# Finer last groups and early modulation reads in stage one, a stepped gate chain, and unscaled down sums in a hybrid retention/mLSTM step on one core

## The chip, the cores and the metric

The kernel runs on one core of a Trainium2 chip. The metric is the device time of one launch in microseconds. A core has a matrix engine (PE), three engines for elementwise work (DVE, ACT, POOL), an engine whose queue issues most transfers (SP), and 16 DMA engines. Each engine takes its instructions in the order of the program and waits at the first one whose inputs or buffers are not ready. PSUM is the memory in which PE leaves its sums.

## The reference

One layer on 384 tokens of 2048 features: 128 context tokens (v = 0) and 256 latent tokens (v = 1). Two conditioning vectors give, through `w_mod`, six vectors for each of them, which shift, scale and gate the layer.

```
mod = silu(c) @ w_mod + b_mod                     # per v: sh1, sc1, g1, sh2, sc2, g2
h   = ln(x) * (1 + sc1) + sh1
proj = h @ w_in                                   # 2048 x 8208, the last 16 columns are gates
ret  = retention in both directions, 4 heads, rope on q and k of the latent tokens
mls  = mLSTM in both directions, 4 heads, with cumulative sums of log_sigmoid(gates)
mix  = concat(ln(ret)*gn*silu(rg), sigmoid(mo)*ln(mls)*gn) @ w_out
x1   = ln(ALPHA * x + g1 * mix) * ln1_g + ln1_b
h2   = ln(x1) * (1 + sc2) + sh2
u, g = split(h2 @ w_up)                           # 2048 x 11008
y    = ln(ALPHA * x1 + g2 * ((silu(conv3(u)) * g) @ w_down)) * ln2_g + ln2_b
```

The final retention and mLSTM states of the context tokens are outputs too. All data are float32. A product is made of three matmuls: each factor is split into a high part `hi` (a copy in the matmul's rounded format, on ACT, L117) and the rest `lo` (a subtraction, on DVE or POOL, L118), and hi*hi, hi*lo and lo*hi are summed in PSUM.

## The kernel before

**Names.** `raw` is a weight tile as it was read, `hi` and `lo` its halves, `ah`/`al` those of the activations, `fah`/`fal` those of the FFN's activations. `psa` are sums of q and k (128 x 384), `psb` sums of v and output gate (128 x 512), `psu` those of `w_up`, `psd` those of `w_down`. A row of features, 128 of 2048, is a "kt"; there are 16.

**Stage one** computes sh1 and sc1 and multiplies heads 0 and 1 while it does. Group (k0, n) covers kt k0 to k0+n-1. For a group, the generator `mods` reads 2 x 16 blocks of `w_mod` (tile `wm`), multiplies them with the conditioning vectors on PE (`modps`, L255), turns the result to columns (`mr`, `modf`, L264) and adds the bias on DVE (`sh`, `sc`, L267). `hs` then makes h (DVE, L337) and splits it (`ah`, `al`). `units` reads `w_in` for the two heads, multiplies the group's kt, and adds the sums to q, k, vx and og (`spill`, L397). In the loop over groups a Stepper advances `mods` of the next group between the units of this one, `finish` drains it, and `hs` of the next group follows after the group's units. Its reads run two tiles ahead (`lag` 2, four `wm` buffers).

**Behind it** come the tables (`cs`, `gnr`, on POOL's queue), rope on heads 0 and 1, the gates, and the other heads. For the gates the weights of the 16 gate columns are read (L552), multiplied with all 16 kt (`gps`, L559, 32 matmuls), summed (`gsum`, L564), passed through log_sigmoid, selected by rows (`gsel`, L575), scanned, and turned to columns (`gcp`). All of this is written in one piece ahead of head 2.

**Vectors by rows.** g1, sh2, sc2 and g2 are computed without PE. `mod_vector` reads 16 tiles `mraw` of `w_mod` for 1024 columns, and DVE multiplies each by the two conditioning values and adds it to `macc` (L283, L286: a pair of operations for each tile); PE sums over the partitions (`modr`). The result goes to DRAM (`modrow`) and is read back. `mods2` is the Stepper for parts 2 to 4, stepped in the projections of heads 2 to 7. `mods5` is that for g2, two blocks of 16 tiles, stepped in the first `ups`.

**Stage three** is the FFN. `ups` multiplies by `w_up`, convolves (L345, L349, L1095) and splits the result; `down` multiplies by `w_down` and `residual` adds g2 times the sum to the residual rows r (L885, L887, L890), with `g2b` as g2 spread over all partitions. The last part, `last_down`, has its own operations on r (L1174 to L1176), and then the final norm (L910 to L916) and the output.

**What sets the order.** The code is written as above, but a scheduler places each instruction on its engine by the readiness it works out, so reads and DVE's work of `mods2` and `mods5` can be placed ahead of the step that issues them in the code. `share_splits(n)` gives every n-th `lo` to POOL. SP's queue holds the reads of weights, of `wm` and of `mraw` in one line.

Of the kernel before, what the change touches and what calls it, by code (L numbers as in the profile page):

```python
# [9 lines left out]
F32 = mybir.dt.float32  # L10
# [72 lines left out]
def hybrid_step(ctx, tc, ca, cb, x_prompt, x_sample, state_ret, state_c, state_n, state_m, c, c_ctx,  # L83
# [294 lines left out]
    groups = [(0, 1), (1, 1), (2, 2), (4, 2), (6, 2), (8, 4), (12, 4)]  # L378
# [20 lines left out]
    def units(k0, n):  # L399
        for h in range(2):  # L400
# [17 lines left out]
    with ExitStack() as p0:  # L418
        xp = pool("xp", 3, p0)
# [10 lines left out]
        def group_raws(gs):  # L430
            return mod_loads(lambda: wmp.tile([P, 2048], F32, tag="wm", name="wm"),
                             [(q, KT // n, part * D + k0 * P, n * P) for k0, n in gs for part in range(2)
                              for q in range(0, KT, KT // n)], 2)

        first_raws, later_raws = group_raws(groups[:1]), group_raws(groups[1:])
# [25 lines left out]
        for kt in range(KT):  # L461
# [6 lines left out]
            if kt == 0:  # L468
                hs(0)
        for g in range(len(groups)):  # L470
            wide = g + 1 < len(groups) and groups[g + 1][1] == 4
            nxt = Stepper(mods(g + 1) if g + 1 < len(groups) else iter(()), 2.0 if wide else 1.2)
# [3 lines left out]
            if g + 1 < len(groups):  # L476
                hs(g + 1)


    with p1:  # L480
        tab = pool("tab", 1, p1, reuse_waits="tile")
        mp = pool("mp1", 3, p1, reuse_waits="tile")
        gx = ExitStack()
        gp = pool("gp", 1, gx, reuse_waits="tile")
        with tc.issue_after(on_pool[0]):
# [18 lines left out]
        pc = pat.tile([P, 64], F32, tag="ps", name="cps")  # L504
        for t in range(3):
            transpose(pc[:, t * 16:(t + 1) * 16], cqr[:, t, :], 16)
        transpose(pc[:, 48:64], n0r, 16)
        nc.vector.tensor_copy(cqw.rearrange("p t f -> p (t f)"), pc[:, 0:48])
        nc.vector.tensor_copy(n0c, pc[:, 48:64])
        ncol = tab.tile([P, 16], F32, name="ncol")  # L510

        def log_sigmoid(dst, x, shape, tg):
            def tmp(n):
                return gp.tile(shape, F32, tag=f"ls{tg}{n}", name=f"ls{tg}{n}")
            e, u, ln = tmp(0), tmp(1), dst
# [12 lines left out]
        log_sigmoid(lgb, lth, [P, 8], "t")  # L528
# [22 lines left out]
        raw = wraw.tile([P, 1024], F32, tag="raw", name="raw")
        nc.sync.dma_start(out=raw[:, :256].rearrange("p (k n) -> p k n", n=16),  # L552
                          in_=wi[:, 8192:8208].rearrange("(k p) n -> p k n", p=P))
        gw = whi.tile([P, 1024], F32R, tag="hi", name="gw")[:, :512].rearrange("p (k s n) -> p k s n", s=2, n=16)
        split(gw[:, :, 0], gw[:, :, 1], raw[:, :256].rearrange("p (k n) -> p k n", n=16), split_engine())
        gps = pmm.tile([32, T], F32, tag="ps", name="gps")
        for kt in range(KT):
            for h in (act_hi[kt], act_lo[kt]):
                nc.tensor.matmul(gps, lhsT=gw[:, kt].rearrange("p s n -> p (s n)"), rhs=h,  # L559
                                 start=kt == 0 and h is act_hi[0], stop=kt == KT - 1 and h is act_lo[kt])  # L560
        gpt = wraw.tile([P, 1024], F32, tag="raw", name="gpt")[:32, :T]
        nc.scalar.copy(gpt, gps)
        gps = pat.tile([16, T], F32, tag="ps", name="gsum")
        nc.tensor.matmul(gps, lhsT=cst[:32, C_SUM:C_SUM + 16], rhs=gpt, start=True, stop=True)  # L564
        gts = gp.tile([16, T], F32, name="gts")
        nc.scalar.activation(gts, gps, AF.Identity, bias=bgc)

        lgs16 = gp.tile([16, T], F32, name="lgs16")
        log_sigmoid(lgs16, gts, [16, T], "g")
        gi = gp.tile([NH, 2, T], F32, name="gi")  # L570
        gf = gp.tile([NH, 2, T], F32, name="gf")
        for d in range(2):
            for o, dst, src in ((8 * d, gi, gts), (8 * d + 4, gf, lgs16)):
                ps = pat.tile([NH, T], F32, tag="ps", name="gsel")
                nc.tensor.matmul(ps, lhsT=ident[:16, o:o + 4], rhs=src, start=True, stop=True)  # L575
                nc.vector.tensor_copy(dst[:, d, :], ps)
# [636 lines left out]
```

## Time and profile before

| | us |
|---|---|
| median of 3 runs | 2083.55 |
| lowest and highest run | 2081.24, 2084.17 |
| the profiled execution, its own time | 2084.25 |
| its span in the trace | 2082.5 |
| stage one, from the first matmul | 4 to about 200 |
| heads 2 to 7 and mixing | about 200 to 960 |
| FFN, up and down | about 978 to 2065 |

In a row of a table of stretches stand the stretch, its length, the busy time and instructions of PE, PEld, DVE, ACT and POOL, PE's granted clock, the DMA engines' busy share and GB/s. In a row of groups stand the line, engine, operation, output and inputs, count, busy time and mean, and the idle time in front with what ended it. In a row of waits stand the engine and its instruction, what it waited for, microseconds in total, the number of waits and the longest. In a timeline a row begins with its start and length; a row "x6" has six instructions in a line.

### The profile page before, as it was taken

What the parts mean: (1) busy time and instruction counts of PE and PEld (TensorE: products, weight loads), DVE (VectorE), ACT (ScalarE), POOL (GpSimd) and SP (SyncE); (2) the same over time, 40 slices, a digit from 0 to 9 for tenths busy, and PEclk for the clock granted to TensorE, in tenths of its full rate; (3) what the DMA queues carried; (4) which work ended last, traced back from release to release, by engine and by line L of the source; (5) the groups of instructions that cost most, each with busy time, mean ns of one, the idle gap of its engine ahead of it and who ended that gap; (6) DMA issues with size and microseconds to landing.
All of it is one profiled execution on the core that took longest, in us unless ns stands there. A gap on an engine that the chain in (4) does not pass through costs nothing.

```text
span 2082.5 us, 26370 instructions
## 1 busy us (share of the span) xinstructions
PE 1993.8 (96%) x10233; PEld 1753.3 (84%) x10233; DVE 1260.7 (61%) x1803; ACT 683.8 (33%) x1035; POOL 287.2 (14%) x245
## 2 busy tenths in 40 slices
PE   6997899999999998997899999999999999999996
PEld 4676678898888876676899988999889998999985
DVE  4657973978688844477949444444444445444458
ACT  4222433243333443235232322333222332233331
POOL 1010332231121201013333100000000000000004
PEclk9998999999999999998999999999999999999998
DMA  9995684888696535833757534444334443434441
GB/s 313 353 318 180 128 157 122 241 214 242 177 206 209 168 104 177 306 116 107 234 162 233 191 126 127 122 124 129 122 122 131 122 124 129 123 112 136 143 152 65
DMA packets 260509, 352.30 MB, mean 169 GB/s; under 512 B 16015, under 2 KB 196560, under 8 KB 259232
## 3 DMA queue, kind: packets, MB, share of 16 engines
q1 hardware_dynamic: 256112, 340.08, 54.7%
q0 software_dynamic: 4272, 10.54, 1.6%
q8 instruction: 80, 1.31, 0.2%
q14 instruction: 45, 0.37, 0.1%
HBM read 343.16 MB, written 7.41 MB: 168 GB/s over the span
## 4 chain that ended last, share of the span: by engine, by line
PE 80%; DVE 10%; DMA 4%; issue 3%; SPq 1%; ACT 1%; POOL 0%; POOLq 0%; DVEq 0%; ACTq 0%
PE psu L184 10%; PE psu L182 10%; PE psu L183 10%; PE psd L192 5%; PE psd L190 5%; PE psd L191 5%; DVE macc L286 4%; PE psb L190 4%; PE psb L191 4%; PE psb L192 3%; PE psa L182 3%; PE psa L184 3%; PE psa L183 3%; PE pso L190 2%; DMA raw<-in_w_in 2%
## 5 line engine op out<-in xcount | busy, mean ns | idle before, releaser
L118 DVE TENSOR_TENSOR lo<-raw,hi 128x1024 fp32r<-128x1024 f32 (+3 forms) x422 | 457.5, 1091 | 540.9 <-ACT hi L117 540.4
L117 ACT CAST hi<-raw 128x1024 fp32r<-128x1024 f32 (+3 forms) x471 | 434.4, 933 | 946.6 <-PE psu L183 335.7
L184 PE MATMUL psu<-ah,lo 128*128 128x384 f32 x1376 | 466.6, 340 | 7.5 <-DVE lo L118 7.5
L182 PE MATMUL psu<-ah,hi 128*128 128x384 f32 x1376 | 466.3, 340 | 2.2 <-DVE y L349 2.2
L183 PE MATMUL psu<-al,hi 128*128 128x384 f32 x1376 | 467.2, 340 | 0.0
L286 DVE SCALAR_TENSOR_TENSOR macc<-mraw,ct,macc 128x1024 f32<-128x1024 f32 x210 | 311.7, 1521 | 14.1 <-DMA mraw<-in_w_mod 14.0
L184 PEld LDWEIGHTS psu<-ah,lo 128*128 128x128 f32 x1376 | 258.9, 188 | 8.8 <-DVE lo L118 8.8
L182 PEld LDWEIGHTS psu<-ah,hi 128*128 128x128 f32 x1376 | 258.9, 188 | 4.4 <-issue 2.5
L183 PEld LDWEIGHTS psu<-al,hi 128*128 128x128 f32 x1376 | 259.0, 188 | 0.2
L182 PE MATMUL psa<-ah,hi 128*128 128x384 f32 x512 | 180.8, 357 | 14.1 <-DVE h L337 10.3
L192 PE MATMUL psd<-hi,fal 128*128 128x512 f32 (+1 forms) x484 | 191.3, 395 | 0.0
L191 PE MATMUL psd<-lo,fah 128*128 128x512 f32 (+1 forms) x484 | 189.5, 392 | 0.0
L190 PE MATMUL psd<-hi,fah 128*128 128x512 f32 (+1 forms) x484 | 188.1, 393 | 0.0
L118 POOL TENSOR_TENSOR lo<-raw,hi 128x1024 fp32r<-128x1024 f32 (+1 forms) x49 | 124.3, 2540 | 398.8 <-ACT hi L117 342.2
L183 PE MATMUL psa<-al,hi 128*128 128x384 f32 x512 | 178.8, 349 | 0.4 <-DVE al L118 0.4
L184 PE MATMUL psa<-ah,lo 128*128 128x384 f32 x512 | 176.8, 349 | 0.9 <-DVE lo L118 0.9
L191 PE MATMUL psb<-lo,ah 128*128 128x512 f32 x384 | 154.6, 403 | 1.1 <-DVE lo L118 1.1
L192 PE MATMUL psb<-hi,al 128*128 128x512 f32 x384 | 153.3, 399 | 0.0
L200 POOL TENSOR_TENSOR brs<-veps,mhalf 128x1 f32<-128x1 f32 x12 | 13.4, 1116 | 984.4 <-DVE veps L198 984.3
L190 PE MATMUL psb<-hi,ah 128*128 128x512 f32 x384 | 148.0, 402 | 0.7 <-DVE q L397 0.7
L182 PEld LDWEIGHTS psa<-ah,hi 128*128 128x128 f32 x512 | 99.3, 194 | 31.8 <-issue 11.0
L191 PEld LDWEIGHTS psd<-lo,fah 128*128 128x128 f32 x484 | 90.9, 188 | 22.3
(298 smaller groups left out, 2355.1 us busy)
## 6 DMA issues: line engine op xcount, KB each, us to landing
raw<-in_w_up SPq DMA_DIRECT2D x168, 512.0 KB, 3.8
mraw<-in_w_mod SPq DMA_DIRECT2D x112, 512.0 KB, 5.1
raw<-in_w_down SPq DMA_DIRECT2D x84, 512.0 KB, 3.6
raw<-in_w_in SPq DMA_DIRECT2D x136, 256.0 KB, 4.6
wm<-in_w_mod SPq DMA_DIRECT2D x32, 1024.0 KB, 8.7
raw<-in_w_in SPq DMA_DIRECT2D x56, 512.0 KB, 7.3
raw<-in_w_out SPq DMA_DIRECT2D x32, 512.0 KB, 4.1
mraw<-in_w_mod SPq DMA_DIRECT2D x8, 1024.0 KB, 7.3
```

The lines of the kernel that those rows point to most:

```text
L117: nc.scalar.copy(dst_hi, src)
L118: mark["lo"] = (eng or nc.vector).tensor_tensor(out=dst_lo, in0=src, in1=dst_hi.bitcast(F32), op=ALU.subtract).ins
L182: nc.tensor.matmul(ps, lhsT=hi[:, s], rhs=ah, start=start, stop=False)
L183: nc.tensor.matmul(ps, lhsT=hi[:, s], rhs=al, start=False, stop=False)
L184: nc.tensor.matmul(ps, lhsT=lo[:, s], rhs=ah, start=False, stop=stop)
L190: nc.tensor.matmul(ps, lhsT=ah[:, t], rhs=hi[:, s], start=start, stop=False)
L191: nc.tensor.matmul(ps, lhsT=ah[:, t], rhs=lo[:, s], start=False, stop=False)
L192: nc.tensor.matmul(ps, lhsT=al[:, t], rhs=hi[:, s], start=False, stop=stop)
L200: mark["pow"] = nc.gpsimd.tensor_tensor(out=out, in0=v[:, :n], in1=mhalf[:, :n], op=ALU.pow).ins
L286: nc.vector.scalar_tensor_tensor(out=acc[:, v, :], in0=raw, scalar=ct[:, kt, v:v + 1], in1=acc[:, v, :], op0=ALU.mult, op1=ALU.add)
```

## The change

Stage one: the groups are (6,3), (9,3), (12,4) in place of (6,2), (8,4), (12,4). The reads of `wm` are of 16, 8, 4 or 4 kt for groups of 1, 2, 3 or 4. From group 4 on they run five tiles ahead, in seven buffers: the four of `wmp`, and three of `wmq`, which lie where the tiles of x were. `hs` of the next group is chained to its `mods` in the Stepper, whose rate is set so that the chain is done within the group.

Gates: the gate weights are read after group 1, and their 32 matmuls follow group by group into one PSUM tile that is held through the stage. The chain from `gsum` to `gcp` is a generator, stepped at half a step for each projection step of heads 2 and on. Its temporaries are free `mix` tiles.

Stage three: POOL takes no `lo` any more, `mods5` is stepped at 0.3 in place of 0.85 and from f0 = 4 on, and is finished after `down(24, 8)`. The down sums are gathered in `acc` without g2: the first as ACT's copy, the middle ones by one DVE addition, the last by an addition, the multiplication by g2 and the addition to ALPHA * r. `g2b` is read back before `ups(32, 7)`. `ln2_g` and `ln2_b` are read into `acc` after the last gather.

```
-    groups = [(0, 1), (1, 1), (2, 2), (4, 2), (6, 2), (8, 4), (12, 4)]
+    groups = [(0, 1), (1, 1), (2, 2), (4, 2), (6, 3), (9, 3), (12, 4)]
...
+        visit = {1: 16, 2: 8, 3: 4, 4: 4}
+        far = 4
...
+        all_raws = [group_raws(groups[:1], 2), group_raws(groups[1:far], 2), group_raws(groups[far:], 5)]
...
         for g in range(len(groups)):
-            wide = g + 1 < len(groups) and groups[g + 1][1] == 4
-            nxt = Stepper(mods(g + 1) if g + 1 < len(groups) else iter(()), 2.0 if wide else 1.2)
+            if g + 1 == far:
+                where[:] = [wmp] * 4 + [wmq] * 3
+            n = groups[g + 1][1] if g + 1 < len(groups) else 1
+            nxt = Stepper(chain(mods(g + 1), hs(g + 1)) if g + 1 < len(groups) else iter(()),
+                          (2 * KT // visit[n] + 5) / 5)
             for _ in units(*groups[g]):
                 nxt.step()
             nxt.finish()
-            if g + 1 < len(groups):
-                hs(g + 1)
+            if g == 1:
+                graw = wraw.tile([P, 1024], F32, tag="raw", name="raw")[:, :256].rearrange("p (k n) -> p k n", n=16)
+                nc.sync.dma_start(out=graw, in_=wi[:, 8192:8208].rearrange("(k p) n -> p k n", p=P))
+                split(gw[:, :, 0], gw[:, :, 1], graw)
+                gate_sums(0)
+            if g > 0:
+                gate_sums(g)
...
+        gating = Stepper(gates(), 0.5)
...
-    share_splits(2)
+    share_splits(0)
...
-    g2b = g2p.tile([P, 2, D], F32, name="g2b")
+    acc = [g2p.tile([P, D], F32, name=f"acc{tt}") for tt in range(NT)]
...
+    def gather(tt, nb, ps, how):
+        s = slice(nb * 512, (nb + 1) * 512)
+        if how == "first":
+            nc.scalar.copy(acc[tt][:, s], ps)
+            return
+        nc.vector.tensor_tensor(acc[tt][:, s], ps, acc[tt][:, s], op=ALU.add)
+        if how == "last":
+            nc.vector.tensor_tensor(acc[tt][:, s], acc[tt][:, s], g2b[:, min(tt, 1), s], op=ALU.mult)
+            nc.vector.scalar_tensor_tensor(out=r[tt][:, s], in0=r[tt][:, s], scalar=ALPHA, in1=acc[tt][:, s],
+                                           op0=ALU.mult, op1=ALU.add)
...
-    mods5 = Stepper(mod_vector(5, pps, mp3, vec_raws(mp3, [(5, j) for j in range(2)])), 0.85)
+    mods5 = Stepper(mod_vector(5, pps, mp3, vec_raws(mp3, [(5, j) for j in range(2)])), 0.3)
     a += ups(2, 10)
-    mods5.finish()
-    share_splits(0)
-    rows_from_dram(g2b, 5)
-    p3m.close()
-    lnp = pool("lnp", 1, p3, reuse_waits="tile")
-    down(0, 12, a, True)
+    down(0, 12, a, "first")
     for f0, n in ((12, 12), (24, 8)):
         down(f0, n, ups(f0, n))
+    mods5.finish()
...
-    l2g = lnp.tile([P, D], F32, name="l2g")
-    l2b = fin.tile([P, D], F32, name="l2b")
-    down(32, 7, a)
+    l2g, l2b = acc[0], acc[1]
+    down(32, 7, a, "last")
```

Three places show what the scheduler makes of it. First, the end of stage one. On DVE before, from the last group's columns `sc` to its h:

```order
L286 SCALAR_TENSOR_TENSOR macc<-mraw,ct,macc 128x1024
L267 TENSOR_TENSOR sc_87<-modf,bmc 128x2x4
L118 TENSOR_TENSOR lo<-raw,hi 128x1024
L286 SCALAR_TENSOR_TENSOR macc<-mraw,ct,macc 128x1024 x2
L337 TENSOR_SCALAR h_1742<-xnt_305,sc_87,sh_86 128x128
```

and after the change:

```order
L397 TENSOR_TENSOR k<-psa,k 128x384 x2
L118 TENSOR_TENSOR lo<-raw,hi 128x4x128 x2
L267 TENSOR_TENSOR sc_87<-modf,bmc 128x2x4
L337 TENSOR_SCALAR h_1740<-xnt_305,sc_87,sh_86 128x128
L337 TENSOR_SCALAR h_1740<-xnt_305,sc_87,sh_86 128x256
```

The macc operations are gone from here; h follows its columns at once, among the units of group (9,3). On SP at the same place, from the last reads for stage one (128x2x256) to head 2 (128x4x256 behind them), before:

```order
L234 DMA mraw<-in_w_mod 128x1024 x2
L141 DMA raw<-in_w_in 128x2x256 x2
L234 DMA mraw<-in_w_mod 128x1024 x6
L552 DMA raw<-in_w_in 128x16x16
L234 DMA mraw<-in_w_mod 128x1024 x4
L141 DMA raw<-in_w_in 128x4x256 x3
L234 DMA mraw<-in_w_mod 128x1024
```

and after:

```order
L141 DMA raw<-in_w_in 128x2x256 x4
L141 DMA raw<-in_w_in 128x4x256 x6
L848 DMA s_2200<-in_state_ret 64x2x256 x2
L848 DMA s_2211<-in_state_ret 64x2x256 x2
L234 DMA mraw<-in_w_mod 128x1024 x3
```

The first six reads of head 2 now stand ahead of every `mraw`, and the first two states too. Second, early stage one on SP, around the reads of group 1 (128x256), before:

```order
L234 DMA wm<-in_w_mod 128x8x256
L141 DMA raw<-in_w_in 128x256
L234 DMA wm<-in_w_mod 128x8x256
L141 DMA raw<-in_w_in 128x256 x3
L234 DMA wm<-in_w_mod 128x8x256
```

and after, where 128x4x384 are reads for group (6,3):

```order
L234 DMA wm<-in_w_mod 128x8x256
L141 DMA raw<-in_w_in 128x256
L234 DMA wm<-in_w_mod 128x4x384
L234 DMA wm<-in_w_mod 128x8x256
L234 DMA wm<-in_w_mod 128x4x384 x2
L141 DMA raw<-in_w_in 128x256 x3
```

Three reads of a far group have moved ahead of weights of group 1. Third, stage three on SP, the first block of `mods5` among the reads of `w_up`, before:

```order
L141 DMA raw<-in_w_up 128x4x256 x4
L234 DMA mraw<-in_w_mod 128x1024 x3
L141 DMA raw<-in_w_up 128x4x256 x5
L234 DMA mraw<-in_w_mod 128x1024
L141 DMA raw<-in_w_up 128x4x256
```

and after:

```order
L141 DMA raw<-in_w_up 128x4x256 x9
L234 DMA mraw<-in_w_mod 128x1024 x3
L141 DMA raw<-in_w_up 128x4x256
L234 DMA mraw<-in_w_mod 128x1024 x2
L141 DMA raw<-in_w_up 128x4x256
```

The block begins five reads later; from there both orders go on with about one `mraw` for each read of `w_up`, 16 in all, and a second block of 16 follows at some distance, in the changed kernel about 24 reads of `w_down` and 57 of `w_up` later.

More of the change, by code (lines that the diff above doesn't have):

```diff
@@ L418, in hybrid_step @@
     with ExitStack() as p0:
[L419 removed]
+        xps = ExitStack()
+        xp = pool("xp", 3, xps, side="right")
         wmp = pool("wmp", 4, p0)
@@ L428, in hybrid_step, with next_raw, group_raws @@
             xs.append(xt)
[L430 to L435, printed above, removed]
+        visit = {1: 16, 2: 8, 3: 4, 4: 4}
+        far = 4
+        where = []
+        def next_raw():
+            home = where[0]
+            where.append(where.pop(0))
+            return home.tile([P, 2048], F32, tag="wm", name="wm")
+        def group_raws(gs, lag):
+            return mod_loads(next_raw, [(q, visit[n], part * D + k0 * P, n * P) for k0, n in gs for part in range(2)
+                                        for q in range(0, KT, visit[n])], lag)
+        where.append(wmp)
+        all_raws = [group_raws(groups[:1], 2), group_raws(groups[1:far], 2), group_raws(groups[far:], 5)]
         def mods(g):
-            raws = later_raws if g else first_raws
-            return chain(*[mod_tensor(part, *groups[g], pat, sbp, raws, KT // groups[g][1]) for part in range(2)])
+            raws = all_raws[(g > 0) + (g >= far)]
+            return chain(*[mod_tensor(part, *groups[g], pat, sbp, raws, visit[groups[g][1]]) for part in range(2)])
         def hs(g):
@@ L468, in hybrid_step, with gate_sums @@
             if kt == 0:
-                hs(0)
-        for g in range(len(groups)):
-            wide = g + 1 < len(groups) and groups[g + 1][1] == 4
-            nxt = Stepper(mods(g + 1) if g + 1 < len(groups) else iter(()), 2.0 if wide else 1.2)
+                for _ in hs(0):
+                    pass
+        xps.close()
+        wmq = pool("wmq", 3, p0, side="right", reuse_waits="tile")
+        gw = sbp.tile([P, KT, 2, 16], F32R, name="gw", bufs=1)
+        gps = pat.tile([32, T], F32, tag="ps", name="gps")
+        def gate_sums(g):
+            for kt in range(groups[g][0], sum(groups[g])):
+                for h in (act_hi[kt], act_lo[kt]):
+                    nc.tensor.matmul(gps, lhsT=gw[:, kt].rearrange("p s n -> p (s n)"), rhs=h,
+                                     start=kt == 0 and h is act_hi[0], stop=kt == KT - 1 and h is act_lo[kt])
+        for g in range(len(groups)):
+            if g + 1 == far:
[3 more added lines that the diff above has]
+                          (2 * KT // visit[n] + 5) / 5)
             for _ in units(*groups[g]):
@@ L475, in hybrid_step @@
             nxt.finish()
-            if g + 1 < len(groups):
-                hs(g + 1)
+            if g == 1:
[5 more added lines that the diff above has]
+                gate_sums(g)
+        gpt = mixp.tile([P, T], F32, tag="mix15", name="gpt")
+        nc.scalar.copy(gpt[:32], gps)
     with p1:
@@ L503, in hybrid_step, with log_sigmoid @@
         n0c = tab.tile([P, 16], F32, name="n0c")
[L504 to L509, printed above, removed]
         ncol = tab.tile([P, 16], F32, name="ncol")
[L512 to L515, printed above, removed]
+        def log_sigmoid(dst, x, e, u):
+            ln = dst
             nc.scalar.activation(e, x, AF.Abs)
@@ L548, in hybrid_step @@
             ret_first(*got)
[L551 to L576, printed above, removed]
```

128 lines of the change are left out of this document (77 added, 51 removed).

## The prediction

> **What bounds the kernel now.** I read the page's totals first, then PE's waits, then a table of stretches, since one share for the span hides stages with different limits.
>
> ```profile
> span 2082.5 us, 26370 instructions
> PE 1993.8 (96%) x10233; PEld 1753.3 (84%) x10233; DVE 1260.7 (61%) x1803; ACT 683.8 (33%) x1035; POOL 287.2 (14%) x245
> PE psa L182 <- DVE h L337: 10.3, 1, 10.3
> PE psu L184 <- DVE lo L118: 7.5, 4, 3.1
> 52.00:104.00 52.00, 51.53 (x353) 36.19 (x352) 35.79 (x91) 14.52 (x34) 3.69 (x2) 1.00 1.05 354
> 156.00:208.00 52.00, 41.27 (x198) 32.04 (x197) 39.08 (x57) 10.73 (x17) 4.98 (x6) 0.87 0.58 180
> 208.00:260.00 52.00, 45.44 (x205) 36.32 (x205) 48.13 (x73) 21.18 (x31) 17.93 (x12) 0.93 0.67 126
> 260.00:312.00 52.00, 47.59 (x243) 41.58 (x242) 38.21 (x63) 19.85 (x39) 17.05 (x20) 0.97 0.88 160
> 988.00:1040.00 52.00, 46.50 (x260) 45.57 (x260) 52.00 (x50) 15.50 (x19) 16.87 (x5) 1.00 0.72 233
> 1092.00:1144.00 52.00, 48.92 (x270) 48.61 (x269) 52.00 (x45) 15.15 (x19) 20.81 (x8) 0.97 0.74 233
> 1300.00:1352.00 52.00, 52.00 (x296) 52.00 (x295) 21.70 (x29) 17.27 (x22) 0.00 (x0) 1.00 0.44 130
> ```
>
> PE's busy ends are modelled, so I count matmuls, not busy time. A stretch with nothing to win is 1300:1352: 296 matmuls of 384 columns in 52 us, 0.176 us each; by columns one of 512 takes 0.234. Most of stage three runs like this, and no edit can win there. Places with fewer matmuls than the pace allows are the end of stage one with head 2 behind it (156 to 312), and the stretch where mods5, the last modulation vector, is summed on DVE (988 to 1144). In both DVE is full or nearly so. Ahead of 156 DMA is at its limit (1.05, 354 GB/s) together with PE.
>
> **End of stage one and head 2: what is lost.**
>
> ```profile
> 170.00:180.00 10.00, 10.00 (x55) 7.25 (x54) 4.22 (x7) 2.84 (x5) 1.56 (x2) 1.00 0.57 179
> 180.00:190.00 10.00, 3.86 (x22) 3.17 (x20) 8.29 (x14) 1.08 (x2) 0.00 (x0) 0.85 0.69 247
> 190.00:200.00 10.00, 5.42 (x15) 4.70 (x16) 10.00 (x14) 1.02 (x2) 0.00 (x0) 0.50 0.65 211
> 200.00:210.00 10.00, 9.78 (x51) 8.66 (x50) 10.00 (x15) 5.69 (x10) 1.89 (x1) 0.96 0.50 158
> 240.00:250.00 10.00, 6.53 (x21) 3.92 (x19) 10.00 (x9) 4.99 (x8) 7.50 (x5) 0.83 1.02 88
> L183 PE MATMUL psa<-al,hi 128*128 128x384 f32 x96 | 35.6, 371 | 0.4 <-DVE al L118 0.4
> L191 PE MATMUL psb<-lo,ah 128*128 128x512 f32 x36 | 14.9, 413 | 0.9 <-DVE lo L118 0.9
> L559 PE MATMUL gps<-al,gw 128*32 128x384 f32 x16 | 5.4, 338 | 0.0
> 188.13 1.28 DVE L286 SCALAR_TENSOR_TENSOR macc<-mraw,ct,macc 128x1024 f32<-128x1024 f32 x1
> 189.32 0.16 DVE L267 TENSOR_TENSOR sc<-modf,bmc 128x8 f32<-128x8 f32 x1
> 189.40 1.22 DVE L118 TENSOR_TENSOR lo<-raw,hi 128x1024 fp32r<-128x1024 f32 x1
> 190.53 2.48 DVE L286 SCALAR_TENSOR_TENSOR macc<-mraw,ct,macc 128x1024 f32<-128x1024 f32 x2
> 192.93 1.25 DVE L337 TENSOR_SCALAR h<-xnt,sc,sh 128x128 f32<-128x128 f32 x4
> ```
>
> First five rows: stretches of 10 us. The next three are groups of PE between 182 and 312, the rest DVE's timeline. PE waits 10.3 us for h of the last group, because modulated columns (sc, L267) and h (L337) stand in DVE's row behind macc pairs and copies. From 180 to 200 PE starts 37 matmuls where neighbours start 51 to 55 per 10 us: about 65 missing, 0.2 us each, 13 us. For 182 to 312, 130 us, the three psa forms (x96 each) need 288 x 0.176 = 51 us, the psb forms (x36 each) 25, the gate sums gps (x32) 6; about 14 I estimate for the small groups of heads, gates and transposes. That is 96, so some 34 us are lost; without the 13 above, **21 us** remain after 208. Two causes show:
>
> ```profile
> 193.04 18.90 SPq L234 DMA_DIRECT2D mraw<-in_w_mod  x6
> 212.03 0.90 SPq L141 DMA_DIRECT2D raw<-in_w_in  x2
> 216.87 19.15 SPq L234 DMA_DIRECT2D mraw<-in_w_mod  x4
> 236.07 2.47 SPq L141 DMA_DIRECT2D raw<-in_w_in  x3
> 253.20 20.25 DMA raw<-in_w_in
> ```
>
> SP issues in order; head 2's weights stand behind four mod reads until 236, then compete, and one read takes 20.25 us on the chain that ended last (240:250 moves 88 GB/s). The gates' chain meanwhile makes PE wait at single places.
>
> **The change part by part.** The sum is made against the profiled run, 2084.25 us (its span 2082.5 and 1.75 around it), 0.7 above the median.
>
> A1, last group's h: steps now make it while group (9,3) is multiplied, and no macc stands ahead of it. Neither the 10.3 us nor the slow matmuls behind it need remain: **-13**. Its bounds: -14, all I can trace, and -5 if h is late by half, since its mod reads must land within one group of three. The gate matmuls only move (6 us of PE either way).
>
> A2, head 2: six weight reads now go ahead of any mraw, and gate sums are complete before. Of 21 us I take back 9: **-9**. It cannot be all, since DVE was at 48.13 of 52 and the macc pairs, some of which stood in 156:208 where DVE had room (39.08), now all lie in heads 2 and 3, beside ropes and splits: the 16 pairs of a block at 1.2 us an op (190.53: two in 2.48) are 38 us. Bounds: -21 and 0 (DVE takes the place of the reads). Steps of the gate chain can wait on each other; DVE orders behind them only short ops, and I put this inside the bounds.
>
> E, early reads: three far reads of 768 KB (2.25 MB) stand ahead of group 1's k weights. At 354 GB/s that is 6.7 us, if those weights are then needed at once. Against it the tables cs and gnr go later on POOL's queue, 1.7 MB or 4.8 us:
>
> ```profile
> wm<-in_w_mod SPq DMA_DIRECT2D x32, 1024.0 KB, 8.7
> cs<-tab_b POOLq DMA_DIRECT2D x1, 1152.0 KB, 6.5
> gnr<-in_gn_ret POOLq DMA_DIRECT2D x1, 512.0 KB, 8.6
> ```
>
> Net **+2**, between 0 and +7. Bytes in all are unchanged. The PSUM bank that gps holds leaves two; a part's modps and modf need just two, so nothing; were a third needed, PE would wait for a copy each time, inside E's upper bound.
>
> B, mods5:
>
> ```profile
> L286 DVE SCALAR_TENSOR_TENSOR macc<-mraw,ct,macc 128x1024 f32<-128x1024 f32 x60 | 98.4, 1680 | 0.0
> L118 DVE TENSOR_TENSOR lo<-raw,hi 128x1024 fp32r<-128x1024 f32 x28 | 37.5, 1338 | 29.7 <-ACT hi L117 29.7
> L118 POOL TENSOR_TENSOR lo<-raw,hi 128x1024 fp32r<-128x1024 f32 x22 | 64.0, 2909 | 144.2 <-ACT hi L117 130.1 <-DVE lo L118 11.8 <-DMA modrow<-mbt 2.3
> 1108.23 1.27 DVE L286 SCALAR_TENSOR_TENSOR macc<-mraw,ct,macc 128x1024 f32<-128x1024 f32 x1
> 1110.56 3.41 DVE L286 SCALAR_TENSOR_TENSOR macc<-mraw,ct,macc 128x1024 f32<-128x1024 f32 x1
> ```
>
> The first three are groups between 978 and 1196. Missing matmuls: 36 in 988:1040 and 26 in 1092:1144, x 0.176 = **11 us**. A macc takes 1.27 us alone and 3.41 beside a POOL split; the mean is 1.68. The slower rate does little: the order still has about one pair for each up read. What counts is POOL's splits coming back. For one up read (24 matmuls, 4.2 us of PE) DVE now does two macc, 3.36, and half a split, 0.67, with convolution and down sums between; after, two macc at 1.27, 2.54, and a whole split at 1.22: 3.76 in place of 4.03. Over the 16 reads of a block that is 4.3 us, against 6.3 and 4.6 lost. So I take **-8**, twice 4.3 rounded down since DVE stays nearly full; bounds -11 and 0.
>
> The Trainium skill, "SBUF — State Buffer", section "Who interferes with whom", states a rule: DVE with two SBUF inputs and a GpSimd op that reads SBUF exclude each other, and the second blocks for the whole instruction. The rows show less: 3.41 - 1.27 is 2.1 us lost to a split, and over all maccs 60 x 0.41 / 22 is 1.1, of a split's 2.9. By the rule the change frees 64 us of DVE for 27 that it takes on, and B would be the whole -11.
>
> D, down sums: first sums are ACT copies, middle ones one DVE add where there were two ops; DVE (21.70) and ACT (17.27) have room there, so nothing. The last gather has three DVE ops instead of two, and its last ones fall in the tail, where DVE is full:
>
> ```profile
> 2060.16 0.68 DVE L1174 TENSOR_TENSOR rtmp<-psd,g2b 128x512 f32<-128x512 f32 x1
> 2060.76 0.68 DVE L1176 BATCH_NORM_STATS2 rst<-r 128x6 f32<-128x512 f32 x1
> l2g<-in_ln_g SPq DMA_DIRECT2D x1, 1024.0 KB, 9.3
> ```
>
> Three more ops, 0.6 us from start to start: **+2**. Bounds 0, and +5: l2g is now read only when its buffer is free, 9.3 us to landing, and the first token tile's scaling on POOL goes later.
>
> Sum: -13 -9 +2 -8 +2 = **-26**, 2058 us.
>
> **The rivals.** *Half of it* (chance 0.25): the freed stretch is DVE's. For it: 48.13 and 52.00 of 52. Head 2 keeps all its loss, A2 = 0, and B gives -5: -13 -5 +4 = -14, 2070. Against it: from 260 on DVE has work for 38.21 of 52, so pairs that are late there find room.
>
> *More* (0.12): each of POOL's splits blocks DVE for its whole 2.9 us, 64 us in all, so that B is the whole -11; and the reads ahead of mraw heal most of head 2, A2 -17, with E at 0: -13 -17 -11 +2 = -39, 2045. Against it: only 1.1 to 2.1 us of a split show as lost, and no part of the order spreads the macc pairs beyond one per read. Its first half is what the rule on SBUF gives.
>
> *Slower* (0.09): far reads starve stage one. SP's queue is one line, DMA is full (1.05), so every far read ahead of a group's weights delays them by its own time. PE is just as full, so it never wins such a delay back. If each of the five group changes after the first costs the 6.7 us of 2.25 MB, that is 33 instead of +2: -26 + 31 = +5, 2089. It decides from four such stalls on. Against it: the reads are only moved, and once they are ahead they ask for no more.
>
> *It does not do what it says*: h's steps are not done when the group ends, since the last mod reads wait for buffers. Then A1 falls to -5 and the rest stays: -18, 2066. It lies within the first rival's reach and takes its chance.
>
> **How the numbers follow.** The forecast has 0.54, from 2050 to 2066; half of it 0.25; more 0.12; slower 0.09. Predicted is 2058. The range goes from 2044, just under more, to 2074, which is half with 4 us of E's and D's upper ends; left out are slower and about half of each of the two tails, 0.2. Runs of this kernel differ by about 0.1%; 0.2%, 4 us, is what a measurement can tell. Faster takes forecast, more and nearly all of half, and is left by most of slower: 0.87; same 0.05, where three or four stalls end near no change; slower 0.08.
>
> **What would show it.** A1: no wait of psa for h above 2 us, granted clock 1.00 through the end of stage one. A2: head 2's raw reads land within 8 us, and PE does not wait for lo. E: no wait of PE for raw, hi or lo before 100 us. B: 988:1144 with no POOL busy time, macc at 1.25 us and 285 matmuls or more per 52 us. D: the tail behind the last matmul 2 us longer. The forecast is wrong if PE's waits for lo in heads 2 and 3 grow, or if stage one's last psb comes later than before by more than the 6 us of gps.

## The result and the profile after

| | us |
|---|---|
| before, median (lowest to highest) | 2083.86 (2081.24 to 2086.26), 4 runs |
| after, median (lowest to highest) | 2065.86 (2062.88 to 2066.45), 4 runs |
| ratio, with its 95% interval | 0.9911 (0.9894 to 0.9928) |
| predicted | 2058, range 2044 to 2074 |
| profiled execution after: time, span | 2066.45, 2064.6 |

The change makes the kernel 18 us faster; 26 were forecast. The range holds the time and the direction is right, so the question is where 8 us of the sum stayed. The totals and PE's waits after:

```profile
span 2064.6 us, 26331 instructions
PE 1985.1 (96%) x10233; PEld 1748.3 (85%) x10233; DVE 1238.6 (60%) x1792; ACT 688.5 (33%) x1048; POOL 235.9 (11%) x225
PE pm L736 <- DVE wk L750: 7.7, 1, 7.7
PE gps L491 <- DVE gw L118: 1.9, 1, 1.9
```

The wait of psa for h is gone. A longer one stands at `pm`, the first step of an mLSTM head's attention, where PE waited 3.1 us before. The stretches of the prediction, after:

```profile
180.00:190.00 10.00, 10.00 (x55) 8.82 (x52) 6.63 (x17) 4.06 (x9) 2.69 (x5) 1.00 0.80 276
190.00:200.00 10.00, 10.00 (x58) 9.43 (x57) 7.96 (x18) 7.89 (x13) 1.96 (x2) 1.00 0.33 105
260.00:312.00 52.00, 50.34 (x229) 41.80 (x228) 52.00 (x64) 18.20 (x29) 27.71 (x16) 0.97 0.83 209
988.00:1040.00 52.00, 49.29 (x270) 48.96 (x270) 43.93 (x52) 16.49 (x21) 0.00 (x0) 0.97 0.72 225
1092.00:1144.00 52.00, 52.00 (x296) 52.00 (x295) 22.29 (x33) 17.22 (x22) 0.00 (x0) 1.00 0.40 122
```

From 180 to 200 PE starts 113 matmuls where it started 37, at full clock. In both stretches of the FFN POOL does nothing, and the second block of adds has moved out of 1092:1144. From 260 to 312 DVE has no idle time, where it had 14 us.

To see how far ahead the changed kernel is at each place, take the same instruction in both. Each row below is one form of PE's matmuls; "a to b" are the starts of the first and the last of it. First before: the last `psb` of stage one (of those up to 240 us), the first `pso`, the first `psu`, the last `psd`; then the same after.

```profile
L192 PE MATMUL psb<-hi,al x48: 390/397/400, 150.7 to 234.5; 128*128 128x512 f32 x48
L190 PE MATMUL pso<-hi,ah x162: 391/398/792, 753.6 to 935.5; 128*128 128x512 f32 x162
L182 PE MATMUL psu<-ah,hi x1376: 333/338/669, 955.9 to 1971.6; 128*128 128x384 f32 x197
L192 PE MATMUL psd<-hi,fal x484: 274/399/399, 1178.1 to 2064.4; 128*128 128x512 f32 x159, 128*128 128x256 f32 x3
```

```profile
L192 PE MATMUL psb<-hi,al x47: 392/397/478, 149.7 to 225.2; 128*128 128x512 f32 x47
L190 PE MATMUL pso<-hi,ah x162: 391/398/794, 739.9 to 921.8; 128*128 128x512 f32 x162
L182 PE MATMUL psu<-ah,hi x1376: 335/338/669, 942.1 to 1950.0; 128*128 128x384 f32 x197
L192 PE MATMUL psd<-hi,fal x484: 279/399/399, 1154.1 to 2042.8; 128*128 128x512 f32 x159, 128*128 128x256 f32 x3
```

The lead is 9.3 us at the end of stage one, 13.7 at the first `pso`, 13.8 at the first `psu`, 21.6 at the last `psd`, and 17.9 at the end of the span. Ahead of `pso` these places are too few to read the terms, because the change moves work across them: 24 of the 32 gate matmuls now lie ahead of the last `psb`, where all lay behind it. So I also take, in both traces, the moment at which PE has streamed the same number of columns. The lead by that measure:

| at this time of the kernel before, us | lead, us |
|---|---|
| 60 | -4.3 |
| 160 | -5.2 |
| 180 | -3.6 |
| 200 | 10.0 |
| 280, in head 2 | 26.3 |
| 420, end of head 3 | 18.0 |
| 580, first `psa` of mLSTM head 2 | 17.9 |
| 640, behind it | 15.4 |
| the first `pso` | 13.7 |

Now the terms can be read. Up to 180 us the changed kernel is 3.6 us behind: E, forecast 2. From 180 to 200 it gains 13.6: A1, forecast 13. From there to the end of head 3 it gains 8.0: A2, forecast 9. This is made of 16 us won by 280 us and 8 given back. Another 4.2 us are given back in mLSTM heads 2 and 3, where the sum has no term. From `psu` to `psd` B gives 7.8, forecast 8. The tail is 3.7 us longer, forecast 2. The run of e2 below is the kernel before up to the FFN, and it is 3.3 us ahead of the trace of before from 60 to 180 us and 1.5 to 1.9 from 300 us on. Against it E costs 6.9, A1 gives 13.2 and A2 10.1; so E and A2 are known to some 3 us.

### The profile page after: what moved, and what is told of

It is laid out like the page before. It is cut to its first block, busy times and chain, and to the rows that moved or that the text cites. A ratio compares the mean times of both kernels' runs of the same rounds, so it can differ in the third digit from the quotient of the medians.

```text
span 2064.6 us, 26331 instructions
## 1 busy us (share of the span) xinstructions
PE 1985.1 (96%) x10233; PEld 1748.3 (85%) x10233; DVE 1238.6 (60%) x1792; ACT 688.5 (33%) x1048; POOL 235.9 (11%) x225
## 4 chain that ended last, share of the span: by engine, by line
PE 82%; DVE 9%; DMA 3%; issue 3%; SPq 1%; POOL 1%; ACT 1%; POOLq 0%; DVEq 0%; ACTq 0%
PE psu L182 11%; PE psu L184 11%; PE psu L183 11%; PE psd L192 5%; PE psd L191 5%; PE psd L190 5%; DVE macc L286 4%; PE psa L182 3%; PE psa L184 3%; PE psa L183 3%; PE psb L191 3%; PE psb L190 3%; PE psb L192 3%; DMA mraw<-in_w_mod 2%; PE pso L190 2%
## 5 line engine op out<-in xcount | busy, mean ns | idle before, releaser
L118 DVE TENSOR_TENSOR lo<-raw,hi 128x1024 fp32r<-128x1024 f32 (+4 forms) x444 | 486.3, 1101 | 533.4 <-ACT hi L117 533.0
L117 ACT CAST hi<-raw 128x1024 fp32r<-128x1024 f32 (+4 forms) x473 | 434.9, 929 | 941.0 <-PE psu L183 355.7
L286 DVE SCALAR_TENSOR_TENSOR macc<-mraw,ct,macc 128x1024 f32<-128x1024 f32 x210 | 285.4, 1396 | 16.1 <-DMA mraw<-in_w_mod 16.0
L190 PEld LDWEIGHTS psd<-hi,fah 128*128 128x128 f32 x484 | 90.9, 188 | 21.1
L192 PEld LDWEIGHTS psd<-hi,fal 128*128 128x128 f32 x484 | 90.9, 188 | 20.6
```

Of the source, the lines that this page charges most:

```text
L117: nc.scalar.copy(dst_hi, src)
L118: mark["lo"] = (eng or nc.vector).tensor_tensor(out=dst_lo, in0=src, in1=dst_hi.bitcast(F32), op=ALU.subtract).ins
L190: nc.tensor.matmul(ps, lhsT=ah[:, t], rhs=hi[:, s], start=start, stop=False)
L192: nc.tensor.matmul(ps, lhsT=al[:, t], rhs=hi[:, s], start=False, stop=stop)
L286: nc.vector.scalar_tensor_tensor(out=acc[:, v, :], in0=raw, scalar=ct[:, kt, v:v + 1], in1=acc[:, v, :], op0=ALU.mult, op1=ALU.add)
```

## The experiments

Single runs are compared by these places in their profiles rather than by the one time. The changed kernel, e1, e3 and e8 are the same program up to the FFN; in their four traces the last `psb` of stage one starts between 225.1 and 225.7, and the first `pso` between 737.0 and 740.4. So a difference of 3 us at `pso` between two runs says nothing.

**e1: POOL's splits again.** In the changed kernel:

```
-    share_splits(0)
+    share_splits(2)
...
     mods5.finish()
+    share_splits(0)
```

> The changed kernel, but with every second lo split of stage three on POOL again until mods5 is done (rate 0.3 kept). Theory: mods5's stretch was slow because POOL's splits stretch DVE's adds; then the two blocks lose some 8 to 11 us again, nearly all of what the change won between the first up matmul and the end of the second block (10 us), and the time goes from 2066 to about 2075. Rival: the later, slower stepping is what helped; then no more than 3 us are lost, 2066 to 2069.

Time 2074.07. **e2: only POOL's splits removed**, in the kernel before:

```
-    share_splits(2)
+    share_splits(0)
```

> The kernel before with one number changed: no lo split of stage three on POOL, rate 0.85 and everything else as it was. Theory (POOL's splits are the cause): 7 to 10 us faster than before, about 2075, the macc at 1.25 us, no POOL busy time between 988 and 1144. Rival (the stepping matters): at most 3 us faster, 2081 to 2084, with DVE full in both blocks and PE still short of its pace.

Time 2074.59, against 2081.01 before in the same set. The groups of both kernels' FFN, e1 then e2: the adds of `mods5`, and POOL's splits where there are any.

```profile
L118 POOL TENSOR_TENSOR lo<-raw,hi 128x1024 fp32r<-128x1024 f32 x56 | 142.6, 2547 | 353.4 <-ACT hi L117 341.3 <-PE modr L293 6.1 <-DMA raw<-in_w_up 6.0
L286 DVE SCALAR_TENSOR_TENSOR macc<-mraw,ct,macc 128x1024 f32<-128x1024 f32 x60 | 98.9, 1688 | 0.0
```

```profile
L286 DVE SCALAR_TENSOR_TENSOR macc<-mraw,ct,macc 128x1024 f32<-128x1024 f32 x60 | 74.7, 1274 | 0.0
L182 PE MATMUL psu<-ah,hi x1376: 335/338/669, 954.3 to 1962.2; 128*128 128x384 f32 x197
L192 PE MATMUL psd<-hi,fal x484: 274/399/399, 1168.7 to 2055.0; 128*128 128x512 f32 x159, 128*128 128x256 f32 x3
```

In e2 the stretch from the first `psu` to the last `psd` is 1100.7 us, as in the changed kernel (1100.7); it was 1108.5. One number gives all of B; the slower rate and the later start give nothing. e1 takes the gain back and more: the stretch is 1111.8 us there, the mean add is 1.69 us where e2 has 1.27, and the time rises by 8 us over the changed kernel's. The mean hides what happens. Of e1's 60 adds 48 take the usual 1.27 us or so, and 12 take 2.76 to 3.42. Each of the 12 begins while POOL is at a split, and each ends 1.08 or 1.09 us after that split, as this pair does:

```profile
985.06 3.01 POOL L118 TENSOR_TENSOR lo<-raw,hi 128x1024 fp32r<-128x1024 f32 x1 [4.79 <-ACT hi L117]
985.73 3.42 DVE L286 SCALAR_TENSOR_TENSOR macc<-mraw,ct,macc 128x1024 f32<-128x1024 f32 x1
```

The split ends at 988.07 and the add at 989.15. So the add gets nearly nowhere until POOL is done. The kernel before has 12 such adds in the FFN too, each ending 1.08 us after its split; e2 and the changed kernel have none.

**e3: h written behind the units; e4: lag 2.** In the changed kernel, apart:

```
-            nxt = Stepper(chain(mods(g + 1), hs(g + 1)) if g + 1 < len(groups) else iter(()),
+            nxt = Stepper(mods(g + 1) if g + 1 < len(groups) else iter(()),
...
             nxt.finish()
+            if g + 1 < len(groups):
+                for _ in hs(g + 1):
+                    pass
```

```
-group_raws(groups[far:], 5)]
+group_raws(groups[far:], 2)]
```

> The changed kernel, but h of the next group is written behind the group's units as before, instead of inside the stepper's chain. Theory: the chain brought most of the 13 to 15 us at the end of stage one, so the wait of psa for h comes back with some 8 us or more and the time is 2074 or above. Rival: what helped is that no macc stands ahead of h any more and that groups are smaller; then the wait for h stays under 3 us and the time within 3 us of 2066.

> The changed kernel with lag 2 in place of 5 for the groups from 4 on (same seven buffers). Theory: the early far reads cost the stall at 55 to 68 us, so that stall shrinks and 2 to 4 us are won there; whether the last group then waits for its mod reads shows what the depth is worth, up to 10 us lost there. Rival: the stall is that of the gate weights in ACT's queue; then it stays at 55 to 68 us.

2066.11 and 2066.46: neither matters. For e3 the order comes out the same as with the chain on every engine, so it makes no difference to the scheduler where h is written, and e3 is in effect a second run of the changed kernel. In e4 the stall at 50 to 70 us stays (PE starts 30 and 36 matmuls in its two stretches of 10 us; the changed kernel 27 and 39). That does not clear the far reads of it: SP's first issues stand in e4 as in the changed kernel, the earliest far reads among them, and differ only from group (12,4) on, far behind the stall. What e4 shows is that the deeper lag from there on is worth nothing.

**e7: gate weights later.**

```
-            if g == 1:
+            if g == 3:
                 graw = wraw.tile([P, 1024], F32, tag="raw", name="raw")[:, :256].rearrange("p (k n) -> p k n", n=16)
...
-                gate_sums(0)
-            if g > 0:
+                for g_ in range(3):
+                    gate_sums(g_)
+            if g > 2:
                 gate_sums(g)
```

> The changed kernel with the gate weights read and split after group 3 instead of group 1, and the sums of groups 0 to 2 caught up there. Theory: their read of 64-byte rows takes 8.7 us and stands in ACT's and DVE's rows ahead of group 2's weights, which makes the stall at 55 to 68 us; then the stall goes, and the time is 3 to 5 us lower, 2061 to 2063. Rival: the stall is made by the far reads ahead of the weights; then it stays, and the time with it.

2062.51. The stretches from 50 to 70 us before, after and in e7, and ACT's row in the changed kernel:

```profile
50.00:60.00 10.00, 10.00 (x65) 5.99 (x63) 6.59 (x21) 1.59 (x6) 0.00 (x0) 1.00 1.03 324
60.00:70.00 10.00, 9.53 (x69) 6.36 (x68) 7.57 (x18) 3.97 (x9) 1.29 (x1) 1.00 1.08 371
```

```profile
50.00:60.00 10.00, 6.46 (x27) 4.65 (x27) 9.01 (x25) 2.84 (x10) 0.00 (x0) 1.00 0.97 315
60.00:70.00 10.00, 7.49 (x39) 4.15 (x40) 3.19 (x9) 2.67 (x7) 1.27 (x1) 0.66 0.73 156
59.90 0.62 ACT L117 CAST hi<-raw 128x512 fp32r<-128x512 f32 x1 [5.63 <-DMA raw<-in_w_in]
63.22 0.40 ACT L117 CAST gw<-raw 128x256 fp32r<-128x256 f32 x1 [2.71 <-DMA raw<-in_w_in]
```

```profile
50.00:60.00 10.00, 8.02 (x59) 5.45 (x60) 8.35 (x24) 3.12 (x10) 0.00 (x0) 1.00 1.09 380
60.00:70.00 10.00, 10.00 (x84) 7.14 (x83) 8.53 (x23) 4.38 (x9) 2.54 (x3) 1.00 1.05 331
```

The gate weights' copy `gw` waits on ACT for its read, and the next weights stand behind it. With the read elsewhere PE starts 143 matmuls in the two stretches instead of 66. The early far reads stand on SP where they stood, so most of this stall is the gate weights' and not theirs. But it is moved and not removed. In e7 the read goes out at 92.6 us, and its copy waits longer than it did:

```profile
104.03 0.41 ACT L117 CAST gw<-raw 128x256 fp32r<-128x256 f32 x1 [8.08 <-DMA raw<-in_w_in]
```

By equal work e7 is 8.7 us ahead of the changed kernel at 80 us and 0.8 at 120. What it keeps is not settled. e11 and e12 below are the same program as e7 up to 240 us and more. They too start more matmuls from 50 to 70 us (130 and 125), though the first 10 us run at a clock of 0.66. But they end stage one at 224.8 and 224.9, where e7 has 222.2 and the changed kernel 225.2. e7's lead of 3.7 us over the changed kernel at the first `pso` (736.2 for 739.9) is not there in e11 (740.2).

**e5 and e6: mods2's adds or its reads taken out.** In the changed kernel, for parts 2 to 4 only. e5 narrows every add to 32 columns:

```
+                        cw = 1024 if part == 5 else 32
-                        nc.vector.scalar_tensor_tensor(out=acc[:, v, :], in0=raw, scalar=ct[:, kt, v:v + 1],
-                                                       in1=acc[:, v, :], op0=ALU.mult, op1=ALU.add)
+                        nc.vector.scalar_tensor_tensor(out=acc[:, v, :cw], in0=raw[:, :cw], scalar=ct[:, kt, v:v + 1],
+                                                       in1=acc[:, v, :cw], op0=ALU.mult, op1=ALU.add)
```

> The changed kernel with each add of mods2 (parts 2 to 4) narrowed from 1024 to 32 columns, so that its work on DVE nearly vanishes while all its reads, waits and buffers stay; g1, sh2 and part of sc2 are left out of the result by that. Theory: the 12 us that the change gives back between 286 us and the first pso matmul (lead of 26 us down to 14) are DVE's, full with the moved adds; then the lead at pso is 24 us or more and the time 2055 or less. Rival: the reads of w_mod among those of w_in cost it; then the lead at pso stays at 14 to 17 us.

e6 reads one tile a block:

```
-                         [(kt, 1, part * D + j * 1024, 1024) for part, j in blocks for kt in range(KT)], 2)
+                         [(kt, 1, part * D + j * 1024, 1024) for part, j in blocks for kt in range(KT if part == 5 else 1)], 2)
...
-                raw = next(raws)
+                raw = next(raws) if part == 5 or kt == 0 else raw
```

> The other half: every block of mods2 reads one tile of w_mod and uses it for all its 16 pairs of adds, so 5 reads in place of 80 with all of DVE's work kept; the sums are then not those of w_mod. DVE theory: the lead at pso stays at 14 to 17 us and the time at 2063 or above. Read theory: the lead at pso is 22 us or more, the time 2058 or less.

Times 2076.36 and 2053.67. The first `pso` of e5 and its wait at `pm`, then the first `pso` of e6, where no such wait is left:

```profile
L190 PE MATMUL pso<-hi,ah x162: 391/398/797, 744.1 to 927.4; 128*128 128x512 f32 x162
PE pm L737 <- DVE wk L751: 11.3, 2, 7.5
```

```profile
L190 PE MATMUL pso<-hi,ah x162: 391/398/793, 725.7 to 907.9; 128*128 128x512 f32 x162
```

With hardly any work on DVE the lead at `pso` falls from 13.7 to 9.5; with all the work and few reads it doubles to 27.9. e6 is the clean one of the two: PE and DVE do the same instructions in the same order as in the changed kernel, and 75 reads are gone. Of the 14.2 us that it wins, 10.4 fall in mLSTM head 2 (by equal work it is 2.1 us ahead of the changed kernel at 580 and 12.5 at 640). So the adds' work alone, which is all there, does not make that loss; their reads have a part in it. e5 has another order on SP, DVE and PE from about 240 us on, since the scheduler places by the durations that it expects. It loses nothing in mLSTM head 2 (18.5 at 580, 19.5 at 640) and then 10 us in the head behind it (9.0 at 680), where PE waits 7.5 us at `pm` while DVE is busy for 6.6 of the 10 us from 660 to 670. So e5 shows that a full DVE is not needed for such a wait; it does not show what the adds cost in the changed kernel. The rows of the changed kernel at the long wait, DVE, POOL and SP:

```profile
557.93 3.42 DVE L118 TENSOR_TENSOR lo<-raw,hi 128x1024 fp32r<-128x1024 f32 x1
...
579.97 1.28 DVE L286 SCALAR_TENSOR_TENSOR macc<-mraw,ct,macc 128x1024 f32<-128x1024 f32 x1 [4.77 <-DMA mraw<-in_w_mod]
...
584.03 0.15 DVE L750 TENSOR_TENSOR wk<-pm,gcol 128x1 f32<-128x1 f32 x1
556.87 3.40 POOL L118 TENSOR_TENSOR lo<-raw,hi 128x1024 fp32r<-128x1024 f32 x1 [22.85 <-ACT hi L117]
568.21 2.72 SPq L234 DMA_DIRECT2D mraw<-in_w_mod  x2
```

`wk` is an operation of 0.15 us, and PE waits 7.7 us for it. It stands on DVE behind an add that waits 4.77 us for its `mraw`; that read was issued at 568.21, when a buffer came free, and landed at 579.88; and ahead of it a split on POOL had held a split on DVE for 3.42 us, until 1.08 us after POOL's end, as with the adds of e1. The granted clock falls with the wait, to 0.52 from 580 to 590 us.

**e10: the heads in another order.**

```
-for h in range(2, NH)] + [(mlstm_proj, mlstm_attn, h) for h in range(NH)]
+for h in (3, 2)] + [(mlstm_proj, mlstm_attn, h) for h in (2, 0, 1, 3)]
```

> The changed kernel with the heads in another order: retention 3, 2 and mLSTM 2, 0, 1, 3. In all runs so far the reads of q and k weights of two stretches (200 to 245 and 535 to 575 us, head 2 of each kind) keep the DMA engines full at 107 to 116 GB/s. Theory A, they are slow by their columns: then the slow stretches move with head 2, to about 290 and 385 us, and the stretch at 200 to 245 is ordinary. Theory B, they are slow by what stands beside them at that time (tables, states): then they stay at 200 and 540. The time may go either way by some us.

2066.32, no gain. Stretches of 20 us of e6, where hardly anything but weights is read, and of e10:

```profile
200.00:220.00 20.00, 20.00 (x99) 17.82 (x98) 10.42 (x19) 7.66 (x10) 5.27 (x4) 1.00 0.93 108
340.00:360.00 20.00, 20.00 (x118) 18.82 (x117) 18.31 (x21) 6.42 (x13) 11.74 (x14) 1.00 0.42 120
540.00:560.00 20.00, 20.00 (x90) 16.19 (x89) 19.68 (x17) 7.30 (x12) 5.22 (x1) 1.00 1.02 116
```

```profile
200.00:220.00 20.00, 20.00 (x100) 17.89 (x99) 10.45 (x19) 7.66 (x10) 5.26 (x4) 1.00 0.50 119
300.00:320.00 20.00, 18.49 (x81) 13.73 (x79) 18.80 (x21) 8.70 (x15) 5.33 (x3) 1.00 1.01 180
400.00:420.00 20.00, 20.00 (x86) 17.16 (x86) 16.28 (x23) 7.47 (x13) 4.52 (x2) 0.86 1.02 239
```

In e6 the slow stretches are the first and the last of the three, where the q and k of retention head 2 and mLSTM head 2 are read. In e10 they move with head 2. So the reads that the prediction meant to free by sending them ahead of `mraw` are slow by themselves: nearly all of the DMA engines for 108 GB/s, where head 3's q and k take 0.42 for 120. The wait at `pm` is 0.5 us in e10, but PE waits 3.8 for a split at 380 to 440 us.

**e9: the old groups.**

```
-(6, 3), (9, 3), (12, 4)]
+(6, 2), (8, 4), (12, 4)]
```

> The changed kernel with the old groups (6,2), (8,4), (12,4) and everything else as changed. Theory: what freed the end of stage one is that no macc stands ahead of the last sc and h on DVE (7.5 us of the 10.3 waited were four rows of macc); then the wait for h stays under 3 us and the time within 3 us of the changed kernel. Rival: the last group's mod reads need the smaller groups to land in time; then PE waits 5 us or more for h or modps at 180 to 195 us.

2069.94. No wait for h: stage one's last `psb` starts at 227.7, 2.5 us later than with the new groups, and the gates' chain has a wait of its own (`gsel` for `lgs`, 4.1 us). The smaller groups are worth some of the 4 us, but the wait for h does not hang on them.

**e8: the scaled sum ahead of the last down.** In the changed kernel, r gets ALPHA * r + g2 * acc ahead of `ups(32, 7)`, and the last gather is the old `residual`:

```
     rows_from_dram(g2b, 5)
+    for nb in range(4):
+        s = slice(nb * 512, (nb + 1) * 512)
+        for tt in range(NT):
+            nc.vector.tensor_tensor(acc[tt][:, s], acc[tt][:, s], g2b[:, min(tt, 1), s], op=ALU.mult)
+            nc.vector.scalar_tensor_tensor(out=r[tt][:, s], in0=r[tt][:, s], scalar=ALPHA, in1=acc[tt][:, s],
+                                           op0=ALU.mult, op1=ALU.add)
...
+        if how == "last":
+            residual(sb3, g2b, tt, nb, ps, False, False)
+            return
```

> The changed kernel with ALPHA * r + g2 * acc formed while w_up's last columns are multiplied, and the last down sums added with two DVE operations (times g2, plus r) as before. Theory: the tail behind the last matmul goes from 21.5 us back to about 18, and the time is 3 to 4 us lower, 2062. Rival: the tail is long because ln2_g and ln2_b are read late into acc; since acc is free earlier here too, the two are told apart by the row of L945: if DVE waits there, it is the read.

2063.54. Its last `psd` and its span:

```profile
L192 PE MATMUL psd<-hi,fal x484: 279/399/399, 1155.0 to 2043.7; 128*128 128x512 f32 x159, 128*128 128x256 f32 x3
span 2061.7 us, 26350 instructions
```

The tail is 18.0 us, as before the change (2082.5 - 2064.4 = 18.1), where the changed kernel has 21.8. So the moved sums make all of the longer tail. How they do it is read from the order and was not tried apart. In the changed kernel the norm of the last token tile but one lies among POOL's work for the tile ahead of it:

```profile
2039.90 1.00 POOL L200 TENSOR_TENSOR brs<-veps,mhalf 128x1 f32<-128x1 f32 x1
2040.93 1.24 DVE L927 SCALAR_TENSOR_TENSOR nm<-bmv,brs 128x1 f32<-128x1 f32 x1 [0.44 <-POOL brs L200]
```

DVE does not wait at L945, so it is not the read of ln2_g: the three more operations, 1.8 us at the prediction's 0.6 each, make the first tile late, and POOL then serves two tiles at once.

**e11 and e12: what can be kept.** e11 joins e7 and e8. e12 takes POOL's splits out of heads 2 to 7 as well:

```
+        share_splits(0)
         heads = [(ret_proj, ret_attn, h) for h in range(2, NH)] + [(mlstm_proj, mlstm_attn, h) for h in range(NH)]
```

> The changed kernel with the gate weights read after group 3 (3.9 us in a single look) and the scaled sum formed ahead of the last down (2.9 us). If the two add up, 2059 to 2060 and a ratio to before of 0.988 or 0.989; if one hides the other, 2062.

> The same with POOL's lo splits taken out of heads 2 to 7 too (every sixth there before). If a split on POOL costs DVE more than on DVE itself, as in mods5's stretch, 1 to 4 us less than without, 2056 to 2058; if DVE is only fuller by it, up to 4 us more, since DVE has no idle time from 240 to 310 us.

| | median (lowest to highest) | ratio to before, 95% |
|---|---|---|
| before, same set | 2084.71 (2083.17 to 2086.64) | |
| e11 | 2059.82 (2058.19 to 2063.41) | 0.9878 (0.9862 to 0.9895) |
| e12 | 2049.96 (2048.61 to 2052.54) | 0.9835 (0.982 to 0.985) |

e11 is 6.0 us below the changed kernel's median, from different sets; e7 and e8 lie 3.4 and 2.3 below the same median, 5.7 together. In the profiled execution of e11, its slowest, the tail is mended but the first `pso` starts at 740.2, so the 3.7 us of e7 did not show there, and how much that half gives is open. e12 is the best kernel of the study, 9.9 us under e11 and more than I expected. The adds and splits of DVE from 200 to 740 us, e11 with POOL's splits and then e12, with e12's first `pso` and its wait at `pm`:

```profile
L286 DVE SCALAR_TENSOR_TENSOR macc<-mraw,ct,macc 128x1024 f32<-128x1024 f32 x150 | 209.7, 1435 | 18.5 <-DMA mraw<-in_w_mod 18.5
L118 DVE TENSOR_TENSOR lo<-raw,hi 128x1024 fp32r<-128x1024 f32 (+1 forms) x101 | 112.6, 1123 | 21.1 <-ACT hi L117 21.0
L118 POOL TENSOR_TENSOR lo<-raw,hi 128x1024 fp32r<-128x1024 f32 (+1 forms) x20 | 59.7, 2991 | 98.2 <-ACT hi L117 65.2 <-ACT dn L790 17.5 <-issue 15.5
```

```profile
L286 DVE SCALAR_TENSOR_TENSOR macc<-mraw,ct,macc 128x1024 f32<-128x1024 f32 x150 | 198.2, 1356 | 10.9 <-DMA mraw<-in_w_mod 10.8
L118 DVE TENSOR_TENSOR lo<-raw,hi 128x1024 fp32r<-128x1024 f32 (+1 forms) x122 | 133.9, 1105 | 31.1 <-ACT hi L117 31.1
L190 PE MATMUL pso<-hi,ah x162: 391/398/792, 727.7 to 909.5; 128*128 128x512 f32 x162
PE pm L737 <- DVE wk L751: 0.6, 1, 0.6
```

DVE is 10 us busier in e12 (332.1 for 322.3 in these two groups), and PE still reaches `pso` 12.5 us earlier than in e11. About half of this, 6.5 us, comes in mLSTM head 2 (by equal work the lead of e12 goes from 21.3 to 25.5 between 580 and 640, that of e11 from 17.4 to 15.1). So it is not the sum of DVE's work that counts here: its adds wait 10.8 us for reads instead of 18.5, and 6.9 us at `pm` shrink to 0.6. e6 loses this wait without the reads, e12 with every read in place and without POOL's splits; so neither makes it alone. The order on the engines differs between e11 and e12 from about 245 us on, so how much of the 9.9 us is the stretching and how much the order was not separated.

## Why the prediction came out as it did

The range holds the time, and the sum came out 8 us too good. Against the profiled runs the missing 8 us are 1.6 of E, 1.0 of A2, 4.2 in the mLSTM heads, 1.8 of D and small rests. The time alone would not have told this: 2066 is also what the prediction gives for "it does not do what it says", where h is late and A1 is -5. That is not what happened.

- **What bounds the kernel** held: stage one's end, the heads behind it and the adds of `mods5` were the places with time to win, and the pace of 296 matmuls in 52 us stands after the change too.
- **A1, -13**: 13.6 us gained where the wait was. The wait for h is gone and the clock stays at 1.00, as the prediction asked. Of its reasons one half fell: neither the chain (e3) nor the groups (e9) are needed for it. What is left of the reasons is that no add stands ahead of `sc` and h on DVE; that was argued from the rows before, and no run put the adds back alone.
- **E, +2**, cost 3.6 to 6.9 us, and its sign failed: before 100 us PE waits twice for `hi`, 1.7 us each, and 1.9 us for `gw`. The prediction put the cost on the far reads. e7 gives most of the stall to the read of the gate weights, for which the sum has no term. The earliest far reads stayed in every run, so their own share was not tried.
- **A2, -9**, gave 8 to 10 us by the end of head 3. The size is right, but in part by luck, since half of what was won went again in a way that the sum does not name. The reads of head 2 do go ahead of every `mraw`, but they do not land within 8 us as the prediction asked: they are slow by their columns (e10), and take 8.3 to 11.8 us. The lead grows all the same to 26 us in head 2, and 8 us of it are lost again by the end of head 3. Something like this loss is in e6 and e12 too (26.0 to 19.2 and 26.6 to 20.5), so neither the reads of `mraw` nor POOL's splits make it; its cause is open.
- **What the sum left out** are 4.2 us in mLSTM heads 2 and 3. It follows the reads and adds of `mods2`, now later in the line, only as far as head 3. Among the slow reads of mLSTM head 2 they make the wait at `pm` 7.7 us, where it was 3.1 (e6, e12). The rival "half of it" had A2 at 0 because DVE is full; that did not happen in heads 2 and 3, and e6 wins 14 us with all of DVE's work in place.
- **B, -8**, was right at 7.8, and for the reason given: e2 alone gives it whole. Of the rest of its 11 us the first block shows something: 988:1040 has 270 matmuls and not the 285 that the prediction asked for. The rule of the Trainium skill, "SBUF — State Buffer", section "Who interferes with whom", says that a DVE operation with two inputs in SBUF and a POOL operation that reads SBUF exclude each other, the second waiting until the first is done. The trace of e1 agrees wherever such an add begins during a split: it ends 1.08 us after the split. The prediction charged the rule to all of POOL's splits, 64 us, and took the smaller mean as a sign against it; but only 12 of the 60 adds meet a split, and e1's and e2's groups give 98.9 - 74.7 = 24 us for them.
- **D, +2**, measured 3.7: the three operations are 1.8 us as worked out, and the rest, by the order, is POOL with two tiles at once. The prediction had put this in its bound of +5.

## What to carry to other kernels

A short operation that PE needed stood here behind an add that waited 4.8 us for a read, and PE waited 7.7; so look at what stands ahead of the small links of a chain, and not only at how full the engine is. Work lent to POOL was not free where DVE worked on SBUF at the same time: an add that met a split took 3.42 us for 1.27, and taking the splits back made this kernel faster in two stages, though DVE did more. A small read of short rows in the line of an engine that feeds PE kept that engine waiting for 2.7 us at one place and 8.1 at another. And follow the lead past the stretch that was changed: 26 us were won here by the middle of head 2, and half of them were gone at `pso`.

## What was not expected of the hardware

Reads of one shape, 128 x 4 pieces of 1 KB of `w_in` for q and k, need twice the DMA time for head 2 that they need for head 3: a share of 0.93 to 1.02 for 108 to 116 GB/s, where head 3's take 0.42 for 120. It follows the columns when the order of the heads changes. Why these columns, 512 behind the start of their block, are slow was not tried.
